# Seven products for the last two row pairs of a down projection, their block sums prepared early

## The chip, the core and the metric

The kernel runs on one core of a Trainium2 chip. The metric is the device time of one execution, in microseconds (us). TensorE (PE in the profile; PEld is its weight load) multiplies, VectorE (DVE) and ScalarE (ACT) do the element-wise work, GpSimd (POOL) and SyncE (SP) issue the DMA transfers: POOL those that accumulate or run on the software queue, SP those on a hardware queue. Each engine works through its own instructions in the order in which the program gives them and waits on semaphores; an issue that waits on SP holds up every later issue on SP.

## The reference

One decoder layer on x of 256 tokens by 2048, float32:

- proj = x @ W_in, split among 8 differential-attention heads and 8 MoBA heads (with 256 tokens MoBA has one block, so it is causal attention), each with partial rotary embedding;
- mix = heads @ W_out; h = LayerNorm(2^0.25 * x + mix);
- u = h @ W_up (2048 by 11264), g and val its halves; act = silu(causal depthwise conv of width 3 over g) * val (256 by 5632);
- out = LayerNorm(2^0.25 * h + act @ W_down), with W_down 5632 by 2048.

## The kernel before

**Precision.** Each float32 operand is split in two float32r parts, `hi` (a ScalarE copy) and `lo` (operand minus hi, on VectorE). A product then takes three: hi by hi, hi by lo, lo by hi. The split tiles come from rings of six `hi` and six `lo` tiles of 128 x 1024 (`splits`). For half of each `k` weight of the differential heads the subtraction is done in another way (`by_dma`): ScalarE writes minus the operand's hi part, and an accumulating DMA on POOL's queue adds the operand.

**Stages.** A list `stream` holds one entry for each weight tile (1 MB): 16 `v` steps, 32 `q`/`k` steps (16 heads, from index `first_q` = 16), 16 `o` steps (from `first_o` = 48), 88 up steps (from `first_u`), and 8 down steps (from `first_d`). Step i multiplies tile i, while the tiles after it are split and those further on are loaded: `begin(i)` and `middle(i)` split tiles i + 2 and i + 3, and `begin(i)` loads tile i + 6. Loads go out on SP into `raw` buffers. There are four, handed out in turn (`raw_tile`, list `turn`); a load waits until the buffer's last reader, the split of the tile that had it before, is done.

**The down projection.** W_down is cut into 22 pairs of 128 rows, p = 0 to 21, and two column halves, n = 0 and 1, of 1024. A pair times a half can be done with eight block products of 128 x 128 by 128 x 512 (24 products with the split), or with seven (21, a Strassen scheme) if sums of the weight blocks and of the activation blocks are made first. Beside the up steps, pairs 0 to 19 run with seven products (the `jobs`): the activations of a pair are spilled to DRAM (`dparts`, `dsums`) and read back for the other half. What is left stands in the eight down steps, called d0 to d7 here:

| step | pair | column half | products |
|---|---|---|---|
| d0, d1 | 20, 21 | n = 0 | 24 each |
| d2, d3 | 20, 21 | n = 1 | 24 each |
| d4 to d7 | 16 to 19 | n = 1 | 24 each, in a last phase ordered by output block |

d0 is the profile's work from 1049.22 us on. In the last phase, token rows 0 to 127 come first: for each of the two column blocks d4, d5, d6, d7 with six products each. Activations of d4 to d7 come back from DRAM (`act_back`, into the tile `back`, and for d7 into `slot`). Column half 0 is finished after d1: `shared_out` and `z_add` add its banks to the residual `z` on VectorE. The gain and bias of the last LayerNorm (2 MB, spread over all partitions) are loaded by `load_gb(2, ...)` into the place of the tile `tslot`. One of the four `raw` buffers serves the jobs during the up steps; it is put back at the head of the turn in the last up step (`turn.insert(0, ...)`), where d4's load takes it.

**What sets the order.** All of it is written out by hand: a dictionary `after` of functions by step, and the order of calls in `up_step`, `begin` and `middle`. A tile with the same tag as an older one waits until every reader and writer of the older one is done, also those that the program issues later.

Of the kernel before, what the change touches and what calls it, by code (L numbers as in the profile page):

```python
# [11 lines left out]
F32 = mybir.dt.float32  # L12
# [39 lines left out]
SEGMENTS = 5  # L52

SEVEN = {"v": ((5,), range(1, 8, 3)), "d": ((), ()), "o": ((3, 6), (3,))}

ORDER = {"v": (1, 0, 2, 3), "d": (0, 1, 2, 3), "o": (2, 0, 1, 3)}

# [5 lines left out]
def hymba_layer(ctx: ExitStack, tc: tile.TileContext, a: dict):  # L63
# [60 lines left out]
            turn.append(n)  # L124
        return keep.tile([P, 2048], F32, name="raw", tag=f"raw{n}"), n

    def load_down(t, p, n):
# [3 lines left out]
        SP.dma_start(b[:, 0:4:3], src[0])  # L131
        SP.dma_start(b[:, 1:3], src[1])

    def load(i):
        if i >= NS or i in loaded or (i, 0) in parts:
            return
        loaded[i] = t = raw_tile()[0]
        if i < 2:

            for k in range(2):  # L140
                load_x(2 * i + k, 2 * i + k + 1)
                for c in range(2):
                    o = i % 2 * 1024 + k * 512
                    SP.dma_start(t[:, c * 1024 + k * 512:c * 1024 + k * 512 + 512], a["w_v"][c, 0][:, o:o + 512])  # L144
            return
        if stream[i][0] == "d":
            load_down(t, *stream[i][1:3])
            return
        for x, y in pieces(i):
            if stream[i][0] == "v":  # L150

                _, p, n, _ = stream[i]
                if n == 0 and x < 1024:
                    load_x(*rows_of(p, x, y))
                o = p % 2 * 1024 + x % 1024
                SP.dma_start(t[:, x:y], a["w_v"][2 * n + x // 1024, p // 2][:, o:o + y - x])
            else:
                SP.dma_start(t[:, x:y], stream[i][3][:, x:y])
# [28 lines left out]
    def split_hi(i, half):  # L187
        if i >= NS or (i, half) in parts:
            return
        o = MOVE_AT if stream[i][0] in "vod" or i - first_u in (0, 1) else 0  # L190
        hi, lo = (splits.tile([P, 1088], F32R, name=n)[:, o:o + 1024] for n in ("hi", "lo"))
        t = loaded[i] if half == 0 else loaded.pop(i)
        ACT.activation(hi, t[:, half * 1024:half * 1024 + 1024], AF.Copy)  # L193
        parts[i, half] = (hi, lo)
        waiting[i, half] = t

    def split_lo(i, half):
        if (i, half) in waiting:
            hi, lo = parts[i, half]
            t = waiting.pop((i, half))  # L200
            DVE.tensor_tensor(lo, t[:, half * 1024:half * 1024 + 1024], hi.bitcast(F32), ALU.subtract)  # L201

    def split_first(i):

# [17 lines left out]

    x2 = keep.tile([P, KT, 2, S], F32R, name="x2", tag="t2")
    xh, xl = x2[:, :, 0], x2[:, :, 1]
    z = keep.tile([P, 2, D], F32, name="z")
    xraw = z.rearrange("p t d -> p (t d)")
# [260 lines left out]
    def load_gb(which, both):  # L487
        for j, n in enumerate(("g", "b")):
            t = both[:, j]
            src = a[f"ln{which}_{n}"]  # L490
            SP.dma_start(t, bass.AP(tensor=src.tensor, offset=src.offset, ap=[[0, P], [1, D]]))
            gb[n] = t
# [37 lines left out]
    def act_back(i):  # L530

        if i >= NS or stream[i][2] == 0 or stream[i][1] >= PT - LATE:
            return
        _, p, _, j = stream[i]
        if "back" not in kept:
            kept["back"] = keep.tile([P, 4, 4, S], F32R, name="back", tag="big")
        t = down_slot()[:, 14:].rearrange("p a (b t) -> p (a b) t", t=S) if i == NS - 1 else kept["back"][:, j % 4]
        POOL.dma_start(t, kept["parts"][p])
# [35 lines left out]
    def act_out(f, u):  # L574
        DVE.tensor_tensor(act_pair(f // 2)[:, f % 2], u, gates.pop(f), ALU.mult)
# [192 lines left out]
                then[m]()  # L768


    side, raw0 = {}, {}

    jobs = [(0, p, 4 * p + 8, 4) for p in range(PART)]
# [101 lines left out]
    for kind, pairs in (("v", VP), ("d", PT)):  # L875
        for n in range(2):
            np_ = pairs - (PAIRED_END + PART * (SEGMENTS - 1) if kind == "d" and n == 1 else 0)
            n7 = 2 * PART if kind == "d" and n == 0 else len(SEVEN[kind][n])
# [34 lines left out]
    def begin(i):  # L913

        urgent(i)
        j = i + 2
        if j < NS and seven(j):
            blocks_raw(j)
            act_sums(j)
        elif j - 1 < NS and seven(j - 1):  # L920
            blocks_sum(j - 1, 1)
            if j - 1 >= VP:
                split(j, 1)
            blocks_hi(j - 1, 1)
# [12 lines left out]
        if i >= first_d:  # L937
            act_back(i + 3)
        load(i + 6)
        pending(i)  # L940
# [21 lines left out]
    def pending(i):  # L962
        for x in after.pop(i, ()):
            if x[0] == LATER:
                x[2](*x[3])

    def done(i):
        for half in range(2):
# [94 lines left out]
    for i in range(first_o):  # L1063
        begin(i)
        if i < first_q:
            run_v(i)
        else:
            run_a(i)
        if i == 8:
            load_consts()  # L1070
        if i == 11:
            lambdas()
        if i == 14:
            SP.dma_start(z, a["x"])
        if i == 14:
            load_table("cos_m")
            load_table("sin_m")
# [33 lines left out]
    for i in range(first_o, last[0]):  # L1111
# [33 lines left out]
    assert not [k for k in after if k <= last[0]], after  # L1145

    h2 = keep.tile([P, KT, 2, S], F32R, name="h2", tag="t2")
    hh, hl = h2[:, :, 0], h2[:, :, 1]
# [235 lines left out]
    def up_step(i):  # L1384
# [24 lines left out]
            early_copies(turning, step)  # L1409
        if carried:  # L1410
            carried.pop()()
        split_hi(i + 2, 0)
        behind = 0 <= turning < SEGMENTS - 1 and step == 3
        if 2 in now and behind:
            r_hi(j, 1, 3)
# [21 lines left out]
            t_hi(3, side["f"][0])  # L1437
        if 0 in new:
            s_lo(1)
        split_hi(i + 2, 1)  # L1440
        if behind:
            up_copy(i)
        if s % 2 == 1 and u is not None:
# [59 lines left out]
        if 2 in now and j == len(jobs) // 2 * 2 - 1:  # L1503

            turn.insert(0, side["raw"][1])
            load(i + 5)
# [19 lines left out]

    for i in range(first_u + 2, first_d):
        up_step(i)
    act_out(FT - 1, up_sum(first_d - 1))
    split_act(first_d + 1, 1)  # L1530

    def z_stats(t, c, w):

# [25 lines left out]
    for i in range(first_d, NS - PAIRED_END):  # L1559
        begin(i)  # L1560
        _, p, n, j = stream[i]
        if i == last[0] - 1:
# [6 lines left out]
            for t in range(2):  # L1569
                for c in range(2):  # L1570
                    z_stats(t, c, (512, 256)[t])
        if seven(i):
            mm_seven(i)
        else:
            for k in range(2):
                mm_d(i, 0, [0, 1], k)
            if n == 0 and p == PT - 1:
                for c in range(2):
                    z_add(0, 0, c, CB[0][c])
            elif i < last[0] - 1:  # L1580
                middle(i)
            for k in range(2):
                mm_d(i, 1, [0, 1], k)
            done(i)
            if n == 0 and p == PT - 1:
                for c in range(2):
                    z_add(0, 1, c, CB[1][c])
                middle(i)
        for k in range(2):
            aparts.pop((i, k))  # L1590

# [171 lines left out]
```

## Time and profile before

| | us |
|---|---|
| median of 3 runs (1104.05 to 1104.23) | 1104.17 |
| the profiled execution | 1104.46 |
| its span, first to last instruction | 1102.7 |
| TensorE busy | 1094.2 |
| VectorE busy | 946.7 |
| ScalarE busy | 721.7 |
| POOL busy | 71.2 |

Times in the profile count from the first instruction. A row of the timeline is: start, duration, engine, line, operation, tiles written <- read, shapes, count, and in brackets the idle time of the engine before it with what ended it. A merged row's duration runs from the first start to the last end. A row of the stretches is: the stretch, its length, the busy time of PE, PEld, DVE, ACT and POOL (with instruction counts), the granted TensorE clock, the busy share of the 16 DMA engines, and GB/s. A row of groups is: line, engine, operation, tiles, shapes, count, then busy us and mean ns of one, then idle time before. A DMA's row shows its issue, not its landing.

### The profile page before, as it was taken

Reading aid. Unit: us, or ns where it says so; the run is one execution under the profiler, and the core shown is the slowest. Engines: PE = TensorE matmul, PEld = TensorE weight load, DVE = VectorE, ACT = ScalarE, POOL = GpSimd, SP = SyncE. Lnnn points to the kernel's source line nnn. Section 1 sums busy time; section 2 is a strip of 40 time slices with the busy share of each in tenths; the row PEclk is TensorE's granted clock in tenths of the full one; section 3 lists DMA queues with packets and bytes.
Section 4 is the critical chain, followed back from the end, with each engine's and each line's share of the span. In section 5 each row is a group of like instructions: output and inputs, shape, how many; then the busy total and the mean of one; then the engine's idle time right before and its main releaser. Section 6 shows DMA issues by size and latency. Waiting matters only on the chain.

```text
span 1102.7 us, 16138 instructions
## 1 busy us (share of the span) xinstructions
PE 1094.2 (99%) x5884; PEld 944.0 (86%) x5884; DVE 946.7 (86%) x1613; ACT 721.7 (65%) x1166; POOL 71.2 (6%) x99
## 2 busy tenths in 40 slices
PE   9999999999999999999999999999999999999997
PEld 6888888888888898888888888888888888888886
DVE  6987778887789979888999989998899988999876
ACT  6765676655475486666666767677776767677652
POOL 0100110000000000000000000000100000000003
PEclk9999999999999999999999999999999999999999
DMA  9899876444467557988988888989898889888772
GB/s 330 271 278 307 253 224 209 156 153 153 160 204 256 185 206 227 289 276 269 311 276 291 284 291 322 305 306 308 283 275 277 303 309 308 298 275 279 209 292 77
DMA packets 64336, 283.54 MB, mean 257 GB/s; under 512 B 6576, under 2 KB 8064, under 8 KB 46464
## 3 DMA queue, kind: packets, MB, share of 16 engines
q1 hardware_dynamic: 53456, 235.57, 58.0%
q0 software_dynamic: 10656, 46.67, 19.0%
q8 instruction: 46, 0.75, 0.3%
q14 instruction: 34, 0.28, 0.1%
q10 hardware_dynamic: 144, 0.26, 0.1%
HBM read 233.69 MB, written 20.97 MB: 231 GB/s over the span
## 4 chain that ended last, share of the span: by engine, by line
PE 98%; DMA 0%; DVE 0%; ACT 0%; SPq 0%; issue 0%; DVEq 0%
PE bank L282 97%; DMA raw<-in_w_v 0%; PE bank L428 0%; PE bank L1162 0%; PE bank L475 0%; DVE z L1611 0%; DVE z L1607 0%; ACT hi L213 0%; DVE st L499 0%; PE bank L1201 0%; DVE z L496 0%; SPq L144 0%; SPq L229 0%; DVE mv L505 0%; ACT ms L1676 0%
## 5 line engine op out<-in xcount | busy, mean ns | idle before, releaser
L282 PE MATMUL bank<-h,hi 128*128 128x512 f32 x1376 | 480.9, 390 | 0.0
L282 PE MATMUL bank<-h,lo 128*128 128x256 f32 x1376 | 387.9, 282 | 0.0
L282 PEld LDWEIGHTS bank<-h,hi 128*128 128x128 f32 x1376 | 258.3, 188 | 54.7
L282 PEld LDWEIGHTS bank<-h,lo 128*128 128x128 f32 x1376 | 259.9, 189 | 3.6
L201 DVE TENSOR_TENSOR lo<-raw,hi 128x1024 fp32r<-128x1024 f32 x173 | 210.4, 1219 | 13.9 <-ACT hi L193 13.6
L193 ACT ACTIVATE hi<-raw 128x1024 fp32r<-128x1024 f32 x173 | 180.6, 1048 | 6.9 <-PE bank L282 6.9
L282 PE MATMUL bank<-x,hi 128*128 128x512 f32 x512 | 182.9, 398 | 0.0
L184 DVE TENSOR_TENSOR lo<-raw,hi 128x1024 fp32r<-128x1024 f32 x115 | 137.5, 1221 | 40.9 <-ACT hi L182 40.7
L182 ACT ACTIVATE hi<-raw 128x1024 fp32r<-128x1024 f32 x123 | 127.6, 1055 | 44.3 <-PE bank L282 21.8
L282 PE MATMUL bank<-x,lo 128*128 128x256 f32 x512 | 144.2, 282 | 0.0
L841 ACT ACTIVATE tslot<-tf 128x512 fp32r<-128x512 f32 x144 | 88.4, 627 | 62.8 <-DVE tf L1477 23.8
L282 PEld LDWEIGHTS bank<-x,hi 128*128 128x128 f32 x512 | 96.2, 188 | 20.6 <-issue 1.0
L844 DVE TENSOR_TENSOR tslot<-tf,tslot 128x512 fp32r<-128x512 f32 x144 | 97.5, 688 | 11.1 <-ACT tslot L841 10.6
L282 PEld LDWEIGHTS bank<-x,lo 128*128 128x128 f32 x512 | 96.8, 189 | 0.2
L1288 ACT ACTIVATE ub<-bank 128x512 f32<-128x512 f32 x86 | 50.7, 590 | 69.7 <-PE bank L282 69.7
L282 PE MATMUL bank<-hi,x 128*128 128x512 f32 x192 | 52.0, 393 | 0.6 <-ACT hi L213 0.6
L282 PE MATMUL bank<-tslot,more 128*128 128x512 f32 x192 | 49.1, 391 | 0.0
L1297 DVE TENSOR_TENSOR ub<-ub 128x256 f32<-128x256 f32 x86 | 36.1, 420 | 12.3 <-ACT ub L1288 12.2
L1426 POOL DMA_DIRECT2D rslot<-raw x18 | 15.8, 879 | 466.6 <-ACT sp L847 466.6
L562 ACT ACTIVATE gc<-ub,vec 128x256 f32<-128x256 f32 x43 | 25.8, 599 | 29.9 <-DVE ub L1297 29.8
L282 PE MATMUL bank<-tslot,sp 128*128 128x512 f32 x180 | 45.0, 391 | 0.0
L282 PEld LDWEIGHTS bank<-hi,x 128*128 128x128 f32 x192 | 36.3, 189 | 8.8 <-ACT hi L213 1.3
(277 smaller groups left out, 1660.5 us busy)
## 6 DMA issues: line engine op xcount, KB each, us to landing
raw<-in_w_u SPq DMA_DIRECT2D x88, 1024.0 KB, 6.9
raw<-in_w_qk SPq DMA_DIRECT2D x32, 1024.0 KB, 5.0
raw<-in_w_d SPq DMA_DIRECT2D x52, 512.0 KB, 6.6
ring<-in_w_d SPq DMA_DIRECT2D x36, 512.0 KB, 6.0
raw<-in_w_o SPq DMA_DIRECT2D x16, 1024.0 KB, 4.9
raw<-in_w_v SPq DMA_DIRECT2D x28, 512.0 KB, 7.3
rslot<-raw POOLq DMA_DIRECT2D x18, 768.0 KB, 7.0
dparts<-rslot SPq DMA_DIRECT2D x20, 512.0 KB, 8.5
```

Source lines behind the costliest of these rows:

```text
L182: ACT.activation(hi[:, s], t[:, x:y], AF.Copy)
L184: DVE.tensor_tensor(lo[:, s], t[:, x:y], hi[:, s].bitcast(F32), ALU.subtract)
L193: ACT.activation(hi, t[:, half * 1024:half * 1024 + 1024], AF.Copy)
L201: DVE.tensor_tensor(lo, t[:, half * 1024:half * 1024 + 1024], hi.bitcast(F32), ALU.subtract)
L282: PE.matmul(out, lhsT, rhs, start=start, stop=stop)
L562: ACT.activation(gates[f], g, AF.Identity, bias=vec[:, C_CB + f:C_CB + f + 1], scale=vec[:, C_W + 2 * FT + f:C_W + 2 * FT + f + 1])
L841: ACT.activation(side["t"][:, 0, j], f, AF.Copy)
L844: DVE.tensor_tensor(side["t"][:, 1, j], f, side["t"][:, 0, j].bitcast(F32), ALU.subtract)
L1288: ACT.activation(t.rearrange("p j t -> p (j t)"), up_bank(i), AF.Copy)
L1297: DVE.tensor_tensor(u[:, 0], u[:, 0], u[:, 1], ALU.add)
L1426: POOL.dma_start(side["r"][:, 1], w[:, 0:3], accum_op=ALU.add)
```

## The change

- d0 and d1 use seven products: 21 instead of 24 (`mm_ready`). The sums of their weight blocks, with their splits, are made during the MoBA heads: for each of the two, from steps `first_q` + 18 and + 25 on, two loads of 0.5 MB, four sums, four splits, and four stores of 0.5 MB to a DRAM tensor (`tsums`). The place of `z` serves as buffer.
- `z` (the residual x, 2 MB) is therefore loaded at step `first_o` - 1 instead of 14.
- To make room on VectorE, half of `k` is split by DMA for the MoBA heads too.
- Before d0 and d1 the prepared blocks are fetched, 2 MB each: d0's on POOL's queue into four `splits` tiles, d1's on SP into `slot` after the up steps. A quarter of their raw weights is no longer loaded. d3's and d5's loads move behind d1's fetch, d4's stays in the last up step.
- d1 is split after the up steps, and the sums of the activations of rows 20 and 21 are made there.
- `act_back` moves from POOL's queue to SP's. `load_gb(2, ...)` moves from the last up step to the end of step d1.
- In step d1, d3's split moves behind the products and the three additions to `z` that follow them.

```diff
-        return kind == "k" and h < NDIFF and half == 1
+        return kind == "k" and half == 1
...
-        POOL.dma_start(t, kept["parts"][p])
+        SP.dma_start(t.bitcast(F32), kept["parts"][p].bitcast(F32))
...
+    def ready_load(c):
+        if c == 0:
+            ready["w"] = keep.tile([P, 4096], F32, name="prep", tag="z")
+            ready["dram"] = dram.tile([len(READY), P, 8, 512], F32R, name="tsums")
+        kind, p, n = READY[c]
+        for k in range(2):
+            SP.dma_start(ready["w"][:, k * 1024:k * 1024 + 1024], a["w_d"][2 * p + 1 - k][:, n * 1024:(n + 1) * 1024])
...
+    for c in range(len(READY)):
+        base = first_q + READY_AT + READY_STEP * c
+        for step, fn, args in ((0, ready_load, (c,)), (2, ready_sums, (0,)), (2.5, ready_hi, (0,)), (3, ready_sums, (1,)),
+                               (3.5, ready_hi, (1,)), (4, ready_lo, (0,)), (5, ready_lo, (1,)),
+                               (5, ready_store, (c, 0)), (6, ready_store, (c, 1))):
+            extra.setdefault(base + step, []).append((fn, args))
...
+    def mm_ready(i, order, then={}):
...
+        pairs = ((0, 0), (0, 1), (1, 0))
+        steps_ = [(m, y) for m in order[:3] for y in pairs]
+        steps_ += [(m, y) for m in order[3:] for y in pairs if y[1] == 0] + [(m, (0, 1)) for m in order[3:]]
...
-        else:
+        elif j != first_d + LATE + 1:
             split(j, 0)
             split(j, 1)
...
+        if i == first_o - 1:
+            z = keep.tile([P, 2, D], F32, name="z")
+            SP.dma_start(z, a["x"])
...
             turn.insert(0, side["raw"][1])
             load(i + 5)
-        load(i + (5 if len(turn) == 3 else 6))
-        if i == first_d - 1:
-            load_gb(2, keep.tile([P, 2, D], F32, name="gb2", tag="ma"))
+        if i < first_d - 2:
+            load(i + (5 if len(turn) == 3 else 6))
+        if i == first_d - 2:
+            ready_fetch(first_d, [splits.tile([P, 1088], F32R, name=n)[:, MOVE_AT:MOVE_AT + 1024]
+                                  for n in ("hi", "hi", "lo", "lo")])
...
     for i in range(first_u + 2, first_d):
         up_step(i)
+    down_act_sums(PT - 2)
     act_out(FT - 1, up_sum(first_d - 1))
     split_act(first_d + 1, 1)
+    ready_fetch(first_d + 1, [down_slot()[:, 0:8]])
+    for j in range(3, 6):
+        load(first_d + j)
+    split_hi(first_d + 1, 0)
...
+    late_sums(PT - 2, keep.tile([P, 4, S], F32R, name="sp", tag="four"))
+    split_hi(first_d + 1, 1)
+    for j in range(2):
+        split_lo(first_d + 1, j)
+    down_act_sums(PT - 1)
+    kept["back"] = keep.tile([P, 4, 4, S], F32R, name="back", tag="big")
+    late_sums(PT - 1, kept["back"][:, 1])
...
-        if seven(i):
-            mm_seven(i)
+        if i == first_d:
+            mm_ready(i, (1, 2, 3, 4, 5, 7, 6))
+        elif n == 0:
+            mm_ready(i, (1, 2, 3, 4, 5, 7, 6), {m: lambda t=t, c=c: z_add(0, t, c, CB[t][c])
+                                                for m, t, c in ((2, 0, 0), (3, 0, 1), (4, 1, 0))})
+            for k in range(2):
+                split(i + 2, k)
+            middle(i)
+            load_gb(2, keep.tile([P, 2, D], F32, name="gb2", tag="ma"))
```

More of the change, by code (lines that the diff above doesn't have):

```diff
@@ L125, in raw_tile, with load_down @@
         return keep.tile([P, 2048], F32, name="raw", tag=f"raw{n}"), n
-    def load_down(t, p, n):
+    def load_down(t, p, n, short=False):
         b = t.rearrange("p (b c) -> p b c", c=512)
         src = [a["w_d"][2 * p + k][:, n * 1024:(n + 1) * 1024].rearrange("p (b c) -> p b c", c=512) for k in range(2)]
-        SP.dma_start(b[:, 0:4:3], src[0])
+        if short:
+            SP.dma_start(b[:, 0], src[0][:, 0])
+        else:
+            SP.dma_start(b[:, 0:4:3], src[0])
         SP.dma_start(b[:, 1:3], src[1])
@@ L146, in load @@
         if stream[i][0] == "d":
-            load_down(t, *stream[i][1:3])
+            load_down(t, *stream[i][1:3], ready_of(i) is not None)
             return
@@ L192, in split_hi @@
         t = loaded[i] if half == 0 else loaded.pop(i)
-        ACT.activation(hi, t[:, half * 1024:half * 1024 + 1024], AF.Copy)
+        w = 512 if half == 1 and ready_of(i) is not None else 1024
+        ACT.activation(hi[:, 0:w], t[:, half * 1024:half * 1024 + w], AF.Copy)
         parts[i, half] = (hi, lo)
-        waiting[i, half] = t
+        waiting[i, half] = t, w
     def split_lo(i, half):
@@ L199, in split_lo @@
             hi, lo = parts[i, half]
-            t = waiting.pop((i, half))
-            DVE.tensor_tensor(lo, t[:, half * 1024:half * 1024 + 1024], hi.bitcast(F32), ALU.subtract)
+            t, w = waiting.pop((i, half))
+            DVE.tensor_tensor(lo[:, 0:w], t[:, half * 1024:half * 1024 + w], hi[:, 0:w].bitcast(F32), ALU.subtract)
     def split_first(i):
@@ L224, in hymba_layer @@
     xh, xl = x2[:, :, 0], x2[:, :, 1]
-    z = keep.tile([P, 2, D], F32, name="z")
-    xraw = z.rearrange("p t d -> p (t d)")
+    xraw = keep.tile([P, 2 * D], F32, name="xraw", tag="z")
     def load_x(k0, k1):
@@ L768, in mm_seven, with ready_of @@
                 then[m]()
+    ready, extra = {}, {}
+    def ready_of(i):
+        kind, p, n, _ = stream[i]
+        return READY.index((kind, p, n)) if (kind, p, n) in READY else None
+    def ready_load(c):
[5 more added lines that the diff above has]
+            SP.dma_start(ready["w"][:, k * 1024:k * 1024 + 1024], a["w_d"][2 * p + 1 - k][:, n * 1024:(n + 1) * 1024])
@@ new lines, in ready_pair, with ready_sums @@
+    def ready_pair(j):
+        w = ready["w"]
+        return (w[:, 2048:3072], w[:, 3072:]) if j == 0 else (w[:, 1024:2048], w[:, 0:1024])
+    def ready_sums(j):
+        b = ready["w"].rearrange("p (b c) -> p b c", c=512)
+        if j == 0:
+            DVE.tensor_tensor(b[:, 4], b[:, 2], b[:, 3], ALU.subtract)
+            DVE.tensor_tensor(b[:, 5], b[:, 3], b[:, 1], ALU.add)
+        else:
+            DVE.tensor_tensor(b[:, 2], b[:, 1], b[:, 4], ALU.subtract)
+            DVE.tensor_tensor(b[:, 3], b[:, 0], b[:, 2], ALU.subtract)
@@ new lines, in ready_hi, with ready_lo, ready_store @@
+    def ready_hi(j):
+        x, hi = ready_pair(j)
+        ACT.activation(hi.bitcast(F32R), x, AF.Copy)
+    def ready_lo(j):
+        x, hi = ready_pair(j)
+        DVE.tensor_tensor(x.bitcast(F32R), x, hi, ALU.subtract)
+    def ready_store(c, j):
+        x, hi = (y.rearrange("p (b c) -> p b c", c=512) for y in ready_pair(j))
+        dst = ready["dram"][c]
+        SP.dma_start(dst[:, 2 * j:2 * j + 2].bitcast(F32), hi)
+        SP.dma_start(dst[:, 4 + 2 * j:6 + 2 * j].bitcast(F32), x)
+    for c in range(len(READY)):
[4 more added lines that the diff above has]
+            extra.setdefault(base + step, []).append((fn, args))
@@ new lines, in ready_fetch @@
+    def ready_fetch(i, tiles):
+        src = ready["dram"][ready_of(i)]
+        if len(tiles) == 1:
+            for j in range(2):
+                SP.dma_start(tiles[0][:, 4 * j:4 * j + 4].bitcast(F32), src[:, 4 * j:4 * j + 4].bitcast(F32))
+            ready[i] = [(tiles[0][:, j], tiles[0][:, 4 + j]) for j in range(4)]
+            return
+        for j, t in enumerate(tiles):
+            POOL.dma_start(t.rearrange("p (b c) -> p b c", c=512).bitcast(F32), src[:, 2 * j:2 * j + 2].bitcast(F32))
+        ready[i] = [tuple(tiles[y][:, x:x + 512] for y in (j // 2, 2 + j // 2)) for j, x in enumerate((0, 512) * 2)]
@@ new lines, in mm_ready @@
+    def mm_ready(i, order, then={}):
+        kind, p, n, _ = stream[i]
+        sh, sl = shares(ready["s", p])
+        (s3, s1), (s2, s4) = ([(sh[j][:, k], sl[j][:, k]) for k in range(2)] for j in range(2))
+        (h0, l0), (h1, l1) = aparts[i, 0], aparts[i, 1]
+        a11, a12, a22 = (h0[:, 0:P], l0[:, 0:P]), (h1[:, 0:P], l1[:, 0:P]), (h1[:, P:], l1[:, P:])
+        w = [weights(i, 512 * b, 512) for b in range(3)]
+        ts = ready.pop(i)
+        ms = {5: (s1, ts[0]), 7: (s3, ts[1]), 6: (s2, ts[2]), 4: (a22, ts[3]), 1: (a11, w[0]), 2: (a12, w[1]), 3: (s4, w[2])}
+        pairs = ((0, 0), (0, 1), (1, 0))
+        steps_ = [(m, y) for m in order[:3] for y in pairs]
+        steps_ += [(m, y) for m in order[3:] for y in pairs if y[1] == 0] + [(m, (0, 1)) for m in order[3:]]
+        final = {m: x for x, (m, _) in enumerate(steps_)}
+        for x, (m, y) in enumerate(steps_):
+            t, c = {2: (0, 0), 3: (0, 1), 4: (1, 0)}.get(m, (None, None))
+            key, dst = ((kind, n, m), MB[m]) if t is None else ((kind, n, t, c), CB[t][c])
+            lhs, rhs = ms[m]
+            mm_count(key, dst, lhs[y[0]], rhs[y[1]])
+            if m in then and x == final[m]:
+                then[m]()
+        done(i)
@@ L877, in hymba_layer @@
             np_ = pairs - (PAIRED_END + PART * (SEGMENTS - 1) if kind == "d" and n == 1 else 0)
-            n7 = 2 * PART if kind == "d" and n == 0 else len(SEVEN[kind][n])
+            n7 = 2 * PART + LATE if kind == "d" and n == 0 else len(SEVEN[kind][n])
             if kind == "d" and n == 0:
@@ L965, in pending @@
                 x[2](*x[3])
+        for fn, args in extra.pop(i, ()):
+            fn(*args)
     def done(i):
@@ L1072, in hymba_layer @@
             lambdas()
-        if i == 14:
-            SP.dma_start(z, a["x"])
         if i == 14:
@@ L1144, in hymba_layer @@
                 at(first_o + 9 + n // 2, z_piece, n // 2, n % 2, bank[n], 1, 512, 1.0)
-    assert not [k for k in after if k <= last[0]], after
+    assert not [k for k in (*after, *extra) if k <= last[0]], (after, extra)
     h2 = keep.tile([P, KT, 2, S], F32R, name="h2", tag="t2")
@@ L1411, in up_step @@
             carried.pop()()
-        split_hi(i + 2, 0)
+        if i < first_d - 1:
+            split_hi(i + 2, 0)
         behind = 0 <= turning < SEGMENTS - 1 and step == 3
@@ L1439, in up_step @@
             s_lo(1)
-        split_hi(i + 2, 1)
+        if i < first_d - 1:
+            split_hi(i + 2, 1)
         if behind:
@@ L1528, in hymba_layer, with late_sums @@
         up_step(i)
+    down_act_sums(PT - 2)
     act_out(FT - 1, up_sum(first_d - 1))
     split_act(first_d + 1, 1)
+    ready_fetch(first_d + 1, [down_slot()[:, 0:8]])
+    for j in range(3, 6):
+        load(first_d + j)
+    split_hi(first_d + 1, 0)
+    def late_sums(p, sp):
+        ready["s", p] = sp
+        side["sh"], side["sl"] = shares(sp)
+        for j in range(2):
+            s_hi(j)
+        for j in range(2):
+            s_lo(j)
+    late_sums(PT - 2, keep.tile([P, 4, S], F32R, name="sp", tag="four"))
+    split_hi(first_d + 1, 1)
+    for j in range(2):
+        split_lo(first_d + 1, j)
+    down_act_sums(PT - 1)
+    kept["back"] = keep.tile([P, 4, 4, S], F32R, name="back", tag="big")
+    late_sums(PT - 1, kept["back"][:, 1])
     def z_stats(t, c, w):
@@ L1576, in hymba_layer @@
                 mm_d(i, 0, [0, 1], k)
[L1577 to L1580, printed above, removed]
+            if i < last[0] - 1:
                 middle(i)
@@ L1584, in hymba_layer @@
             done(i)
[L1585 to L1588, printed above, removed]
         for k in range(2):
```

3 lines of the change are left out of this document (2 added, 1 removed).

## The prediction

> **What bounds the kernel now.** I read the page first (busy shares, chain), then the chain in order of time, then TensorE's timeline around the changed steps, then the engines' stretches, and last the queues.
>
> ```profile
> span 1102.7 us, 16138 instructions
> PE 1094.2 (99%) x5884; PEld 944.0 (86%) x5884; DVE 946.7 (86%) x1613; ACT 721.7 (65%) x1166; POOL 71.2 (6%) x99
> ...
> 402.17 691.11 PE bank L282 x3708
> 1093.28 0.02 issue
> ...
> 1049.22 0.62 PE L282 MATMUL bank<-hi,ends 128*128 128x512 f32 x2
> ...
> 1070.98 0.39 PE L282 MATMUL bank<-hi,back 128*128 128x512 f32 x1
> ```
>
> TensorE is the bound: from 402 us its products follow each other without a hole until 1093.28. So each product taken away is worth its start-to-start distance, and each wait put in front of TensorE costs its full length. The two rows at 1049.22 and 1070.98 are the starts of d0 and d4 (names as in the section on the kernel); between them lie four steps of 24 products: 21.76 / 96 = 0.2267 us each.
>
> **Products removed.** d0 and d1 go from 24 to 21 products: 6 x 0.2267 = -1.36 us. That is all the change can bring. In the new order d1 would start at 1053.98, d2 at 1058.74, d3 at 1064.18, and the last phase at 1069.62, whose first six products are d4's; d5's activations ("back") are read after them, at 1070.98.
>
> **MoBA heads: sums made early.** Rows: one pair of steps with a MoBA head, one with a differential head (which already splits half of `k` by DMA), columns us, busy PE, PEld, DVE, ACT, POOL, clock, DMA share, GB/s; then the groups that price the additions.
>
> ```profile
> 234.87:247.61 12.74, 12.74 (x78) 11.37 (x76) 10.36 (x22) 6.43 (x12) 0.00 (x0) 1.00 0.47 165
> 155.20:167.50 12.30, 12.30 (x78) 11.02 (x76) 9.99 (x26) 9.02 (x23) 1.61 (x2) 1.00 0.74 218
> ...
> L184 DVE TENSOR_TENSOR lo<-raw,hi 128x1024 fp32r<-128x1024 f32 x25 | 30.0, 1220 | 9.5 <-ACT hi L182 9.5
> L182 ACT ACTIVATE hi<-raw 128x1024 fp32r<-128x1024 f32 x24 | 25.4, 1057 | 10.8 <-issue 8.1 <-PE bank L282 2.7
> L676 DVE TENSOR_TENSOR tf<-raw 128x512 f32<-128x512 f32 x1 | 0.7, 684 | 0.0
> ```
>
> VectorE loses 8 subtractions (8 x 1.22 = 9.8 us) and gets per row pair 4 sums and 2 subtractions (4 x 0.684 + 2 x 1.22 = 5.2), 10.4 in all: even. ScalarE gets 8 + 4 copies of 1.06 us, 12.7 us over 102 us, with 6.3 us free in every 12.74. The DMA engines get 8 accumulates of 0.5 MB, 2 MB of loads and 4 MB of stores, at a share of 0.47. In the row of 155.20 such accumulates run at a share of 0.74 and TensorE is busy for all 12.30 us. Cost 0; cover: VectorE's 2.4 us and the DMA engines' half. Without cover it would be at most the third sum's wait for its load, about 1 us.
>
> **z's load moved from step 14 to step 47.** It is 2 MB, waits on SP for the stores of the last prepared block, and stands ahead of the `w_o` loads.
>
> ```profile
> 301.20 0.33 SPq L158 DMA_DIRECT2D raw<-in_w_o  x1
> ...
> 321.27 0.86 POOL L675 DMA_DIRECT2D oslot<-raw  x1 [16.01 <-ACT oslot L674]
> ...
> raw<-in_w_qk SPq DMA_DIRECT2D x32, 1024.0 KB, 5.0
> ```
>
> The load behind it is issued at 301.20 and first read some 2 us before the accumulate of 321.27. It lands within 5.0 us unhindered; 2 MB ahead of it cost some 5.3 us at 400 GB/s. It lands at about 311: hidden, with 8 us left. `z` itself is first read in step 55. Cost 0.
>
> **The turn from up to down steps.** The sums of rows 20 and 21 and the split of d1 now run after the last up step.
>
> ```profile
> 1043.28 1.05 ACT L1523 ACTIVATE rslot<-raw 128x1024 fp32r<-128x1024 f32 x1
> 1044.23 0.70 ACT L596 ACTIVATE ends<-ring 128x256 fp32r<-128x256 f32 x2
> 1048.24 0.42 ACT L596 ACTIVATE ah<-ring 128x256 fp32r<-128x256 f32 x1 [0.95 <-DVE ring L575]
> 1048.68 1.28 ACT L1544 ACT_TABLE_LOAD   x1
> ...
> L850 DVE TENSOR_TENSOR sp<-sf,sp 128x256 fp32r<-128x256 f32 x4 | 1.7, 418 | 0.0
> L855 DVE TENSOR_TENSOR sf<-ring 128x256 f32<-128x256 f32 x1 | 0.4, 415 | 0.0
> L856 DVE TENSOR_TENSOR sf<-sf,ring 128x128 f32<-128x128 f32 x1 | 0.3, 291 | 0.0
> L857 DVE TENSOR_TENSOR sf<-ring,sf 128x128 f32<-128x128 f32 x1 | 0.3, 291 | 0.0
> ```
>
> ScalarE after 1048.6 (each row's start to the next start: 0.95 for 1024 columns, 0.35 for 256): d1's first half, then the two sums of row 20, ready at 1050.3. TensorE wants them after six products, at 1050.58. VectorE's two subtractions (0.42 each) end at about 1050.8 against 1051.04. Cost 0, margin 0.2; if missed, below 0.5 us.
>
> **Fetches.** The rows: POOL's last accumulate of the up steps, its time to landing (median), and the last use of h2's step.
>
> ```profile
> 1035.64 0.88 POOL L1426 DMA_DIRECT2D rslot<-raw  x1 [29.42 <-ACT sp L847]
> ...
> rslot<-raw POOLq DMA_DIRECT2D x18, 768.0 KB, 7.0
> ...
> 1046.49 0.85 PE L282 MATMUL bank<-tslot,rslot 128*128 128x512 f32 x3
> ```
>
> d0's 2 MB stand on POOL in place of d3's load, behind that accumulate, so they move from 1042.6. With 0.5 MB of spilled activations and d4's 1 MB beside them, 3.7 MB at 0.4 MB per us, all has landed at 1051.8; the last block is wanted after 17 products of d0, at 1053.1. d1's 2 MB leave SP when h2 is free (1046.49, the up products' end). `hi` is wanted at 1056.0 and `lo` at 1057.8; behind the above they land at about 1054.4 and 1057.0. Cost 0, ends 0 and 2 us.
>
> **Down steps: the queue of SP.** Here I expect the loss. The rows: SP's issues before, POOL's issues before, then VectorE.
>
> ```profile
> 1047.38 0.33 SPq L491 DMA_DIRECT2D gb<-in_ln_g  x1
> 1058.12 0.38 SPq L131 DMA_DIRECT2D raw<-in_w_d  x1
> ...
> 1049.90 1.61 POOL L538 DMA_DIRECT2D back<-dparts  x3 [13.38 <-PE bank L282]
> ...
> 1055.73 2.36 DVE L184 TENSOR_TENSOR lo<-raw,hi 128x1024 fp32r<-128x1024 f32 x2 [2.20 <-ACT hi L182]
> 1063.55 1.28 DVE L1319 TENSOR_TENSOR z<-z,bank 128x512 f32<-128x512 f32 x2
> 1071.54 2.35 DVE L184 TENSOR_TENSOR slot<-raw,slot 128x1024 fp32r<-128x1024 f32 x2
> 1073.81 2.35 DVE L184 TENSOR_TENSOR end<-raw,end 128x1024 fp32r<-128x1024 f32 x2
> 1069.70 2.01 ACT L182 ACTIVATE end<-raw 128x1024 fp32r<-128x1024 f32 x2 [0.28 <-DMA raw<-in_w_d]
> ```
>
> Before, the four activation fetches leave an otherwise idle POOL at 1049.9, and d7's load is issued at 1058.12, when d3's split has ended (1055.73 + 2.36). After, SP issues in this order: d3, d5, d6, back of d4, d7, gain and bias (2 MB), back of d5, of d6, of d7. And d7's load changes its buffer. d4 is now loaded before d3, so the turn of the four buffers gives d7 the one of d4: the load waits for d4's split, and everything behind it on SP waits too.
>
> When is d4 split? VectorE, in order: sums and split of d1 and the sums of row 21 until about 1054.4 (1.22 + 0.69, 1.0, 0.84, with ScalarE's copies between); d2's split behind ScalarE's table load, until 1058.8; three additions to z (0.64 each) until 1060.7; d3's and d4's splits, 4 x 1.18, until 1065.4. The lower end comes from TensorE: the third addition needs product 18 of d1, at 1053.98 + 18 x 0.2267 = 1058.06; one addition and four splits later it is 1063.4. I take 1065.4, since ScalarE is serial there.
>
> What is then on the way? d7's megabyte, 5.0 us by the row above: 1070.4. Gain, bias and d5's half megabyte, 2.62 MB, at the rate of these stretches:
>
> ```profile
> 1055.00:1060.00 5.00, 5.00 (x24) 4.14 (x23) 3.56 (x4) 1.65 (x2) 0.00 (x0) 1.00 1.06 408
> 1060.00:1065.00 5.00, 5.00 (x24) 4.14 (x23) 4.93 (x7) 2.49 (x3) 0.00 (x0) 1.00 1.09 397
> ```
>
> 2.62 / 0.402 = 6.5 us: d5's activations land at 1076.9 and TensorE wants them at 1070.98. Stall 5.9 us. The ends: release at 1063.4 gives 3.9; a d7 load as slow as before (1058.12 to 1069.70, 11.6 us) gives 12.5. I take 5.9, because the engines have little else left by then. d6's and d7's activations follow 1.3 us apart, as fast as TensorE uses them (1.36).
>
> **The clock after such a hole.** Rows: the first products, the last ones, the last window.
>
> ```profile
> 1.20 4.45 PE L282 MATMUL bank<-idle 128*128 128x512 bf16 x10 [1.20 <-DVE idle L902]
> 5.08 1.64 PE L282 MATMUL bank<-hi,x 128*128 128x512 f32 x4
> 6.56 0.62 PE L282 MATMUL bank<-lo,x 128*128 128x512 f32 x2
> ...
> 1093.11 1.88 PE L282 MATMUL bank<-z,ident 128*128 128x512 f32 x4
> ...
> 1097.00:1102.00 5.00, 0.00 (x0) 0.00 (x0) 1.26 (x2) 0.86 (x2) 0.00 (x0) 0.61 0.58 211
> ```
>
> The mean of 0.61 in the last window is full clock for about 1.1 us and half after, so the clock fell at 1098.1, 3.1 us after the dense products ended (1094.99). A hole of 5.9 us is longer. Coming back, the first ten products of the kernel start 0.388 us apart and the next four 0.37, against 0.2267: 14 products lose 1.6 to 2.2 us. I take 1.9.
>
> [...]
>
> **The sum.** -1.36 + 5.9 + 1.9 = +6.4 us. The profiled run took 1104.46 us with a span of 1102.7, 0.29 over the median of 1104.17; against the median: 1110.6 us, +0.6%.
>
> **Rivals.**
> 1. The hole comes but the clock stays full: +4.5, 1108.7 us. For it: 5.9 is only twice 3.1, and one early activation shortens it.
> 2. The activations are in time, VectorE is not. Before, d7's first `lo` is ready at 1075.0 (1073.81 + 1.2) and wanted at 1075.3. After, VectorE still has eight additions (0.64) and d5's split (2.35) behind 1065.4 and reaches d6 at 1072.9, 1.3 later than before, while TensorE is 1.36 earlier: a stall of 1.3 + 1.36 - 0.3 = 2.4, 1105.2 us. This decides only if the activations land before 1073.4.
> 3. Not slower: d7's load finds its buffer free before 1070.98 - 6.5 - 5.0 = 1059.5, and nothing is late: 1102.8 us. Against it: product 18 of d1 ends at 1058.06 and d3's and d4's splits are yet to come.
> 4. d1's fetch is late by 2 us as well: d4's split moves along, 1112.6 us.
>
> **Chances.** Forecast 0.44, rival 1 0.25, rival 2 0.08, rival 3 0.10, rival 4 with larger stalls 0.10, and 0.03 for a gain above the six products that I can't name. 0.2% (2.2 us) is about what a measurement of this kernel tells from no change. Slower is forecast, rivals 1 and 4: 0.79; within: rivals 2 and 3, 0.18; faster 0.03. The range goes from just under rival 2 (1104.4) to rival 4 with a late release (1114.0); the forecast with rival 1 alone spans 1106.7 to 1113.
>
> **What would show it.** TensorE idle for some 6 us near 1071, waiting for "back"; a granted clock below 1 just after; SP's back issues behind gain and bias, after a d7 load issued near 1065; no idle TensorE in the MoBA heads or between 1049 and 1069. It is wrong if d7's load is issued before 1060, or if the hole stands elsewhere.

## The result: slower by 0.8%, and the profile after

The changed kernel takes 1112.51 us (1111.35 to 1116.44), the kernel before, on the same chip, 1104.27 (1104.05 to 1104.6): a ratio of 1.0079, 95% interval 1.0064 to 1.0095. Forecast were 1110.6 us and a range of 1104.4 to 1114.0. The profiled execution of the changed kernel took 1111.35 us, 6.89 more than the profiled one before; it is the quickest of the six, so what the median has above it stands in no trace.

One correction comes first, since it bears on the reading. In the listing of the change, `load(i + 5)` behind `turn.insert(0, ...)` stands as kept, and the text says that d4's load stays in the last up step. In the changed kernel that line is gone: d4's load moves behind d1's fetch too, and the order there is d3, d4, d5. So d3, not d4, takes the buffer that is put back at the head of the turn, and d7's load waits for d3's split. The prediction was built on the wrong order.

The page of the changed kernel (span and engines), and from its chain of waits the pieces around the longest one (start us, us, what):

```profile
span 1109.6 us, 16224 instructions
PE 1095.4 (99%) x5878; PEld 943.8 (85%) x5878; DVE 947.8 (85%) x1626; ACT 732.9 (66%) x1182; POOL 78.3 (7%) x107
...
1066.47 11.61 DMA back<-dparts
1078.08 0.14 issue
1078.21 22.42 PE bank L288 x114
```

PE's busy time is much as before, yet the chain no longer runs through TensorE alone: it crosses a transfer of d5's activations that takes 11.61 us. TensorE's timeline in the heads, at d2's start and in the last phase (start us, us, line, operation, count, and in brackets the idle time and what ended it):

```profile
272.24 0.28 PE L288 MATMUL bank<-x,lo 128*128 128x256 f32 x1
273.79 0.70 PE L434 MATMUL bank<-ident,e 128*128 128x128 f32 x3 [1.28 <-DVE e L428]
...
1060.56 1.06 PE L288 MATMUL bank<-hi,ends 128*128 128x512 f32 x2 [0.58 <-DVE z L1410]
...
1073.02 0.39 PE L288 MATMUL bank<-hi,back 128*128 128x512 f32 x1
1078.21 0.77 PE L288 MATMUL bank<-hi,back 128*128 128x512 f32 x1 [4.81 <-DMA back<-dparts]
1078.78 0.63 PE L288 MATMUL bank<-lo,back 128*128 128x512 f32 x1
1079.21 1.05 PE L288 MATMUL bank<-hi,back 128*128 128x512 f32 x2
```

Three waits, of which one was forecast. Between starts, and less the usual distance of 0.2267 us in the down steps, they cost 1.6 us in the heads, 1.1 at d2 (two gaps) and 4.97 in the last phase. Then the products are 0.427 us apart (1079.21 to 1080.06 for two) until about 1081.2, some 1.5 us lost. The stretches say the same in their columns of granted clock, DMA share and GB/s (the last three):

```profile
1070.00:1075.00 5.00, 3.41 (x16) 2.48 (x14) 4.93 (x7) 2.33 (x3) 0.00 (x0) 1.00 1.01 419
1075.00:1078.00 3.00, 0.00 (x0) 0.00 (x0) 3.00 (x3) 0.00 (x0) 0.00 (x0) 0.97 1.01 404
1078.00:1081.50 3.50, 3.29 (x8) 2.68 (x9) 2.70 (x7) 0.31 (x1) 0.00 (x0) 0.54 0.17 65
```

Added up: the six products -1.36, heads +1.6, d2 +1.1, hole +4.97, clock +1.5, a start that was 0.57 earlier in this execution and an end some 0.4 shorter: +6.8 of 6.89 us. Between these places TensorE has no hole, as in these two stretches (the first after the heads' wait, the second to the end of the up steps):

```profile
275.00:400.00 125.00, 124.99 (x651) 107.12 (x650) 110.87 (x186) 74.47 (x122) 4.57 (x6) 1.00 0.71 234
400.00:1040.00 640.00, 640.00 (x3461) 556.15 (x3460) 575.08 (x918) 448.66 (x675) 39.19 (x57) 1.00 0.85 285
```

And SP's queue in the down steps (timeline, issues only):

```profile
1059.84 0.38 SPq L137 DMA_DIRECT2D raw<-in_w_d  x1
...
1060.83 0.38 SPq L544 DMA_DIRECT2D back<-dparts  x1
1063.90 0.38 SPq L137 DMA_DIRECT2D raw<-in_w_d  x1
...
1064.85 0.42 SPq L497 DMA_DIRECT2D gb<-in_ln_g  x1
1065.31 1.11 SPq L497 DMA_DIRECT2D gb<-in_ln_b  x1
1066.47 0.91 SPq L544 DMA_DIRECT2D back<-dparts  x2
```

In order: d6's weights, d4's activations, then 3 us of nothing while d7's load waits for d3's split, then d7, gain, bias, and only then the activations of d5 and d6.

### The profile page after: what moved, and what is told of

It is laid out like the page before. It is cut to its first block, busy times and chain, and to the rows that moved or that the text cites. A ratio compares the mean times of both kernels' runs of the same rounds, so it can differ in the third digit from the quotient of the medians.

```text
span 1109.6 us, 16224 instructions
## 1 busy us (share of the span) xinstructions
PE 1095.4 (99%) x5878; PEld 943.8 (85%) x5878; DVE 947.8 (85%) x1626; ACT 732.9 (66%) x1182; POOL 78.3 (7%) x107
## 5 line engine op out<-in xcount | busy, mean ns | idle before, releaser
L208 DVE TENSOR_TENSOR lo<-raw,hi 128x1024 fp32r<-128x1024 f32 x173 | 209.2, 1212 | 14.1 <-ACT hi L200 13.7
L190 DVE TENSOR_TENSOR lo<-raw,hi 128x1024 fp32r<-128x1024 f32 x107 | 128.0, 1220 | 37.0 <-ACT hi L188 36.6
L932 DVE TENSOR_TENSOR tslot<-tf,tslot 128x512 fp32r<-128x512 f32 x144 | 97.5, 687 | 11.2 <-ACT tslot L929 10.7
```

The source lines that it names most:

```text
L190: DVE.tensor_tensor(lo[:, s], t[:, x:y], hi[:, s].bitcast(F32), ALU.subtract)
L208: DVE.tensor_tensor(lo[:, 0:w], t[:, half * 1024:half * 1024 + w], hi[:, 0:w].bitcast(F32), ALU.subtract)
L932: DVE.tensor_tensor(side["t"][:, 1, j], f, side["t"][:, 0, j].bitcast(F32), ALU.subtract)
```

## The experiments

Times are medians; each ratio is against the kernel before, measured beside it. Each edit is to the changed kernel unless it says otherwise.

### 1. Gain and bias behind the activations (e1_gain_last)

```diff
-            load_gb(2, keep.tile([P, 2, D], F32, name="gb2", tag="ma"))   # end of step d1
+            load_gb(2, keep.tile([P, 2, D], F32, name="gb2", tag="ma"))   # after act_back(last[3])
```

> The changed kernel with one issue moved: gain and bias are loaded behind the activations of d5 to d7 on SP instead of ahead of them. Theory (order on SP's queue makes the hole): d5's activations have 2.1 MB less ahead of them, 5.2 us at 0.4 MB per us, and land at about 1072.9 where TensorE wants them at 1073.2; the hole of 4.97 us shrinks to less than 1 us, the clock stays full (1.5 us more), so 1112.5 - 6.5 = about 1106 us. Rival (the added 3.5 MB make the last transfers late in any order): the hole moves to d7's weights or to gain and bias, and the time stays above 1110 us.

1106.56 us (1105.97 to 1110.26), ratio 1.003 [1.0019, 1.004]. One line moved on SP's queue takes away 6 of the 8.2 us: the hole and the half clock are gone (the mean clock of the profile is 0.999, of the changed kernel's 0.996). What is next in line there is a split of d7 (TensorE's timeline):

```profile
1077.63 1.43 PE L288 MATMUL bank<-end,slot 128*128 128x512 f32 x5 [0.60 <-DVE end L190]
```

Between starts it costs 0.77. With heads 1.7 and d2 1.1 that is -1.36 + 3.6 = +2.2, and the profiled execution is at 1106.42, 1.96 above the one before.

### 2. The activations back on POOL's queue (e2_back_on_pool)

```diff
-        SP.dma_start(t.bitcast(F32), kept["parts"][p].bitcast(F32))
+        POOL.dma_start(t, kept["parts"][p])
```

> The changed kernel with the activations of d4 to d7 on POOL's queue again. Theory (order on SP): they are issued before 1060 and land before 1070; no hole at the activations; the VectorE splits of d6 and d7 come next and cost 0 to 2.4 us; 1105.5 to 1108 us. Rival (volume): they take turns with SP's loads, so d7's load lands 1.5 MB / 0.4 = 3.9 us later than now (1071.8), TensorE waits for its split some 3 us, the clock may fall, 1109 to 1111 us.

1112.99 us (1111.53 to 1115.14), ratio 1.0081 [1.0065, 1.0096]: nothing is gained, and the theory that a queue of their own makes the activations timely and the kernel quick fell. They are timely; other things are late. POOL's issue, ScalarE's copy of d3, and two of TensorE's waits (timelines):

```profile
1053.31 1.59 POOL L544 DMA_DIRECT2D back<-dparts  x3 [9.10 <-ACT hi L200]
...
1065.23 2.01 ACT L188 ACTIVATE hi<-raw 128x1024 fp32r<-128x1024 f32 x2 [4.52 <-DMA raw<-in_w_d]
...
1076.97 0.50 PE L288 MATMUL bank<-lo,back 128*128 128x512 f32 x1 [0.97 <-DVE lo L190]
...
1081.90 2.50 PE L288 MATMUL bank<-slot,back 128*128 128x512 f32 x5 [3.27 <-DVE slot L190]
```

2 MB of activations are on the way from 1053 on, beside SP's weights, and d3's weights are the ones that lose: ScalarE waits 4.52 us for them. Behind the last of these waits five products take 2.50 us, against 1.43 in experiment 1's row, and in the heads the clock halved (0.50 from 276 to 279 us, last section); the mean clock of the profile is 0.993. Between starts the two stretches cost some 4.5 us of this profile's 10.7 above the one before.

### 3. The hole filled with products that serve for nothing (e3_filled_hole)

```diff
+            if c == 0 and i == last[1]:      # last phase, ahead of d5
+                for _ in range(18):
+                    mm(MB[1], aparts[last[0], 0][0][:, 0:P], weights(last[0], 0, 512)[0], True, True)
```

> The changed kernel with 18 products more (18 x 0.227 = 4.1 us) into an unused bank, between d4's and d5's products of the last phase, where TensorE stands idle for 4.97 us. Theory (the clock falls in the hole and costs 1.5 us after it): the granted clock stays full, the products behind the hole start 0.227 us apart instead of 0.427, and the time falls by about 1.5 us, to 1111 us. Rival (the slow products cost nothing, since the activations of d6 and d7 are awaited anyway): the time stays at 1112.5 us.

1111.02 us (1109.59 to 1113.28), ratio 1.0063 [1.0048, 1.0078]; the profiled execution 1109.59, 1.76 below that of the changed kernel. TensorE's timeline:

```profile
1072.74 4.47 PE L288 MATMUL bank<-hi,back 128*128 128x512 f32 x19
1077.85 0.47 PE L288 MATMUL bank<-hi,back 128*128 128x512 f32 x1 [0.64 <-DMA back<-dparts]
1078.16 0.39 PE L288 MATMUL bank<-lo,back 128*128 128x512 f32 x1
```

The activations come at the same time, but the product behind them is short (0.39, not 0.63) and the next ones are 0.227 apart; the mean clock of the profile is 0.999, against 0.996. So the clock's share of the loss is about 1.5 us, as expected; the two ranges of times overlap, so it rests on the rows.

### 4. The sums in the heads, one to two steps earlier (e4_sums_earlier)

```diff
-READY_AT, READY_STEP = 18, 7
+READY_AT, READY_STEP = 16, 8
```

> The changed kernel with the preparation of rows 20 and 21 begun at steps first_q + 16 and + 24 instead of + 18 and + 25, so that the second pair's load is issued two steps after the first pair's last store and on a step whose load does not wait for an accumulate. Theory (VectorE stands 5.7 us for the second pair's load, which makes the one wait of TensorE in the heads): TensorE's wait of 1.6 us at 272 goes, VectorE's wait falls below 2 us, 1112.5 - 1.6 = 1110.9 us. Rival (the heads lack VectorE or DMA time as a whole): the wait turns up at another head, and the time stays at 1112.5 us.

1112.56 us (1112.18 to 1112.62), ratio 1.0074 [1.0057, 1.0091]: no gain. The wait at 272 us goes, and one of 1.3 us comes around 220 us, where the first pair's sums now fall among the last differential heads and VectorE has nothing free. Of the 1.6 us that were expected some 0.4 are left in TensorE's heads, and the mean clock of this profile is 0.995, against 0.996 of the changed kernel's.

### 5. The heads' load ahead of the step's weight load (e5_load_first, with 1)

```diff
+        for fn, args in extra.pop(("first", i), ()):   # ready_load
+            fn(*args)
         load(i + 6)
```

> e1 (gain and bias last) with one more edit: the preparation's two loads per row pair go out on SP at the head of their step, ahead of that step's weight load, which waits for an accumulating DMA. Theory (VectorE's 5.7 us for the second pair's load come from that place in SP's queue): the loads of row 21 are issued some 4 us earlier, near 258 us, VectorE waits below 2 us and TensorE's wait of 1.5 us at 272 is gone: 1106.5 - 1.5 = 1105.0 us, and the spread of the runs (1106 to 1110 in e1) narrows, if it comes from the clock falling in that wait. Rival (e4: the heads lack VectorE time, the wait only moves): a wait of 1 us or more stays between 210 and 300, 1106 us.

1106.33 us (1105.31 to 1108.83), ratio 1.0024 [1.0015, 1.0034]: the same as experiment 1 within the intervals. The theory was that the second pair's load is late because it stands behind a weight load that waits for a split by DMA. SP's own waits from 255 to 265 us (us in total, times, longest), first of the changed kernel, then of this one:

```profile
SPq L164 <- DMA lo<-raw: 10.7, 1, 10.7
SPq L789 <- DMA tsums<-prep: 0.7, 1, 0.7
```

```profile
SPq L789 <- DMA tsums<-prep: 12.1, 2, 11.3
```

With the wait in front taken away, the load waits just as long for something else: the first pair's stores to DRAM, out of the buffer that it wants to fill. It was a second wait, hidden behind the first, and the load goes out at 262.2 us in the one and 262.4 in the other. That is why the heads lack cover. TensorE's wait there was 0.9 us in this profile against 1.7 in experiment 1's, but 2.0 in experiment 7's, which has the same load. In the changed kernel VectorE then stands in the sum (timeline), and the head's own `e` behind it:

```profile
270.91 0.69 DVE L798 TENSOR_TENSOR prep<-prep 128x512 f32<-128x512 f32 x1 [5.74 <-DMA prep<-in_w_d]
```

### 6. The order at the turn and in d1 (e6_turn_order, with 1)

```diff
+        elif i == first_d:                      # d2's copies only
+            split_hi(j, 0)
+            split_hi(j, 1)
...
-    ACT.activation(root, eps, AF.Sqrt)
...
+            ACT.activation(root, eps, AF.Sqrt)  # behind step d0
...
+            def then_z(m, t, c):                # in step d1
+                z_add(0, t, c, CB[t][c])
+                if m == 3:
+                    for k in range(2):
+                        split_lo(first_d + 2, k)
```

> e1 with two edits at the turn: d2's subtractions stand behind the first two additions to z on VectorE instead of ahead of all three, and the activation table's load stands behind d2's copies on ScalarE. Theory (VectorE's order makes d2's wait of 1.1 us and, through its backlog, the 0.77 us at d7): both waits go, VectorE reaches d6 some 1.9 us earlier, 1106.5 - 1.9 = 1104.6 us. Rival (VectorE has too much to do there in any order): d2's wait turns into a wait for d2's subtractions or grows at d7, 1106 us or more.

1107.7 us (1105.25 to 1108.98), ratio 1.0031 [1.0018, 1.0044], where about 1104.6 was expected. The wait at d2 is gone, which shows its cause: VectorE did d2's subtractions, which waited for ScalarE, ahead of the additions that free TensorE's banks. (The table load, which held ScalarE up for 1.28 us, moved with them; the two edits were not separated.) The wait at d7 is gone as well, but that shows less, since the new wait below may give VectorE the time. In the changed kernel (VectorE's timeline):

```profile
1057.45 2.36 DVE L190 TENSOR_TENSOR lo<-raw,hi 128x1024 fp32r<-128x1024 f32 x2 [2.03 <-ACT hi L188]
1059.73 1.88 DVE L1410 TENSOR_TENSOR z<-z,bank 128x512 f32<-128x512 f32 x3
```

But TensorE, now earlier, waits 1.2 us for d5's activations, and the profiled execution lost 2.5 us to the wait in the heads, with a half clock behind it (0.51 from 276.0 to 279.5 us).

### 7. 5 and 6 together (e7_both)

> The edits of e1, e5 and e6 together. Theory: the changed kernel's waits were all made by the order of its queues, so what is left is the six products: 1104.2 - 1.36 = 1102.8 us, just below the kernel before, with the spread of the kernel before. Rival (some of the waits belong to the added work itself): above 1104.2 us.

1106.45 us (1104.25 to 1107.58), ratio 1.0022 [1.0013, 1.0031]; 1102.8 was expected. In its profile 2.0 us stay in the heads (the load of experiment 5 is no earlier) and 1.6 for d5's activations.

### 8. What the products are worth (e8_six_less: the kernel before, six products of d0 and d1 left out)

```diff
+        if (kind, n, t, c, k) == ("d", 0, 1, 1, 1):
+            continue
```

> The kernel before with six products of d0 and d1 left out and nothing else changed: it leaves out one of the eight blocks of each of these two pairs. Theory (six products are all that there is to gain): between 1102.8 us (1104.2 - 6 x 0.2267) and, since VectorE's last splits were only 0.3 us ahead of TensorE at d7, 1103.9 us. Rival (there is more to gain than the products' own time): below 1102.5 us.

1102.83 us (1102.52 to 1103.19), ratio 0.9989 [0.998, 0.9999]. 1.2 of 1.36 us arrive when nothing is added in return. This is the most that the change could bring.

### 9. The heads' work spread out (e9_heads_spread, with 1 and 6)

```diff
-READY_AT, READY_STEP = 18, 7
+READY_AT, READY_STEP = 16, 8
-        for step, fn, args in ((0, ready_load, (c,)), (2, ready_sums, (0,)), ...
+        for step, fn, args in ((0, ready_load, (c,)), (3.5, ready_sums, (0,)), ...
```

The loads go out as in experiment 4, but the first sum follows 3.5 steps behind its load instead of 2, the stores 6.5 and 7 instead of 5 and 6.

> Gain and bias last (e1), the order at the turn (e6), and another timetable in the heads instead of e5's edit: the first row pair's loads at step 32 with its sums from 35.5 on, the second's loads at step 40 with its sums from 43.5 on, so that the first pair's last stores are issued two steps ahead of the second pair's loads into the same buffer. Theory (the second load waits for those stores to land, 11 to 13 us; VectorE then waits for the load): no wait of TensorE above 0.3 us between 200 and 310; what is left is the wait for d5's activations seen in e6 (1.2 us) and e7 (1.6): 1104.1 - 1.36 + 1.5 = 1104.2 us, with a spread below 1 us. Rival (VectorE is short of time in the heads): a wait of 0.5 us or more at 220 or 272, 1105 us and more.

1104.3 us (1103.51 to 1106.38), ratio 1.0004 [0.9995, 1.0013]. The heads' wait is gone (stretch of this kernel):

```profile
260.00:275.00 15.00, 15.00 (x91) 13.43 (x90) 11.36 (x24) 9.77 (x16) 0.86 (x1) 1.00 0.95 327
```

So the load's late landing was its cause: it goes out 3.9 us earlier (258.35 against 262.21) and has 1.5 steps more until the sum, and VectorE doesn't stand in the sum. Experiment 4, with the early load alone, still had 1.8 us of that wait on VectorE, but none of TensorE there; what the spreading adds is the place at 220 us, where the first pair's sums no longer cost TensorE anything. The version is 3.4 us below experiment 6, which differs only in the timetable. Left is the wait for d5's activations:

```profile
1072.74 0.47 PE L288 MATMUL bank<-hi,back 128*128 128x512 f32 x1 [1.70 <-DMA back<-dparts]
```

### 10. d5's activations ahead of d7's load (e10_d5_first, with 9)

```diff
-        if i >= first_d:
+        if i >= first_d and i != first_d + 2:
             act_back(i + 3)
+        if i == first_d + 1:
+            act_back(i + 4)
```

> e9 with one more edit: d5's activations go out on SP ahead of d7's load instead of behind it. Theory A (only the order on SP is left): d5's wait goes and nothing takes its place, 1102.8 to 1103.2 us. Theory B (VectorE is the next bound there: it has the sums and splits of d1 to do in the turn and reaches d6 and d7 some 1.5 us later than in the kernel before): d5's wait goes, a wait of 1 to 2 us for the splits of d6 or d7 takes its place, and the time stays at 1104.2 us.

1103.9 us (1103.44 to 1104.56), ratio 0.9998 [0.9989, 1.0007]: level with the kernel before, and the best version found. Neither theory named what followed: d5 is in time, and d6's activations are late.

```profile
1073.12 1.62 PE L288 MATMUL bank<-slot,back 128*128 128x512 f32 x6 [0.94 <-DMA back<-dparts]
```

A likely reason is in the last two columns (DMA share, GB/s) of the stretches around the down steps, first of the kernel before, then of this one:

```profile
1060.00:1070.00 10.00, 10.00 (x46) 8.29 (x45) 9.40 (x12) 6.69 (x8) 0.00 (x0) 1.00 0.82 306
1070.00:1075.00 5.00, 5.00 (x24) 4.14 (x23) 4.97 (x7) 1.91 (x3) 0.00 (x0) 1.00 0.01 2
1040.00:1078.00 38.00, 38.00 (x176) 31.73 (x175) 28.78 (x40) 19.12 (x25) 2.14 (x4) 1.00 0.75 268
```

```profile
1060.00:1070.00 10.00, 10.00 (x46) 8.28 (x45) 9.86 (x12) 6.44 (x7) 0.00 (x0) 1.00 1.03 387
1070.00:1075.00 5.00, 4.06 (x18) 2.77 (x16) 4.97 (x7) 2.01 (x2) 0.00 (x0) 1.00 1.04 423
1040.00:1078.00 38.00, 37.06 (x170) 30.36 (x169) 30.73 (x48) 20.34 (x28) 0.47 (x1) 1.00 0.99 376
```

Before, 268 GB/s over 38 us are 10.2 MB, and by 1070 the engines are done. After, 376 GB/s are 14.3 MB, and they are full to the end: 4.1 MB more in the same 38 us take up the whole spare quarter.

### 11. d6's activations ahead of d7's load too (e11_backs_first, with 10)

```diff
+        if i == first_d + 1:
+            for j in range(4, 7):
+                act_back(first_d + j)
```

> e10 with d6's activations ahead of d7's load too (1 MB more ahead of it than in e9, 2.6 us). Theory A (only the order on SP is left): no wait above 0.3 us in the last phase, 1102.8 to 1103.1 us. Theory B (the DMA engines are full from 1045 to 1075 in e10, so what goes first makes the next thing late): d7's weights land some 1.3 us later than in e10, TensorE waits 0.5 to 1.5 us for d7's split in place of the 0.94 us for d6's activations, and the time stays at 1103.4 to 1104.2 us.

1104.93 us (1104.01 to 1106.68), ratio 1.0007 [0.9998, 1.0016]. If only the order were wrong, this would be the fix. Instead the waits move on to what now comes behind (TensorE's timeline, then ScalarE's copies of d7):

```profile
1072.59 1.43 PE L288 MATMUL bank<-slot,back 128*128 128x512 f32 x5 [0.45 <-DVE slot L190]
1074.37 0.47 PE L288 MATMUL bank<-end,slot 128*128 128x512 f32 x1 [0.34 <-DMA slot<-dparts]
1075.43 1.45 PE L288 MATMUL bank<-end,slot 128*128 128x512 f32 x5 [0.59 <-DVE end L190]
...
1073.06 2.01 ACT L188 ACTIVATE end<-raw 128x1024 fp32r<-128x1024 f32 x2 [4.45 <-DMA raw<-in_w_d]
```

Of the orders tried, none puts everything in time. That the volume is too much for the stretch in any order is argued from the full shares, not shown. Nor is it the only bound: the first of these waits, 0.6 us between starts, is for VectorE, which waited for nothing before it and was busy for 14.25 of the 14.50 us from 1059.10 on.

## Why the prediction was right, and where it was not

**What held.** The direction, and the mechanism behind its largest part: d5's activations stand on SP behind d7's load and behind gain and bias, TensorE waits for them in the last phase, and the clock halves (0.50 from 1078 to 1081 us). Experiment 1 shows the queue's order as the cause, experiment 3 the clock. The six products are worth what was said (1.36 by count, 1.2 in experiment 8). `z`'s load (SP waits 9.1 us at its line, TensorE not at all), the turn and both fetches cost 0.

**The hole: 5.9 forecast, 4.97 measured, by errors that cancel.** The step "d7's load changes its buffer" failed: it waits for d3's split, not d4's, and went out at 1063.90, not 1065.4. The step "the engines have little else left by then" failed too: from 1063.90 to the landing at 1078.08, at some 0.406 MB per us (402 to 419 GB/s), 5.8 MB moved, not the 3.62 counted. Some 1.3 MB of the rest were d6's weights and d4's activations, still on the way; most of the remainder, some 0.8 MB, were the activations of d6 and d7, issued behind d5's but moved beside them (after 1078.08 the engines had only 0.2 MB left). So the activations landed at 1078.08 instead of 1076.9. And TensorE wanted them at 1073.25 instead of 1070.98, since it had lost time in two places by then. That the two errors nearly cancel is luck.

**The heads: cost 0 forecast, 1.6 measured.** The sign "no idle TensorE in the MoBA heads or between 1049 and 1069" did not hold, here and at d2. The failed step is the cover, "VectorE's 2.4 us and the DMA engines' half", taken as means over a step. I had priced its loss, "the third sum's wait for its load, about 1 us", but not asked what holds the load back: it reuses a buffer whose stores are 11 us under way. The stretches show that the half wasn't there either: from 255 to 270 us the share was 0.98.

```profile
255.00:270.00 15.00, 15.00 (x90) 13.39 (x89) 8.86 (x19) 8.51 (x18) 0.86 (x1) 1.00 0.98 317
```

**d2: not in the sum at all, 1.1 measured.** The prediction had the order on VectorE ("d2's split behind ScalarE's table load, until 1058.8; three additions to z until 1060.7") and used it only for d3's and d4's splits. It didn't ask who waits for those additions; TensorE does.

**The clock: 1.9 forecast, 1.5 measured.** It took effect for seven to eight products, not fourteen. Rival 1 (full clock, 1108.7) is out.

**The other rivals.** Rival 2, VectorE late for d7 once the activations are in time, is what experiment 1 showed, at 0.77 us at d7 where 2.4 were worked out, and experiment 11 again, at 0.6 us at d6. Rival 3's 1102.8 was reached by no version that does the added work, though the activations were made timely: something else was late each time. Rival 4, d1's fetch late, didn't occur. The forecast was 1.9 us under the median: the two terms taken as 0 are worth 2.7, and the hole and the clock together came out 1.3 smaller; the remaining 0.5 is the balance of start, end and the spread of the runs, which no term covers.

## What to carry to other kernels

A load that is put on an in-order queue takes over every wait in front of it (here the 3 us that d7's load waits ahead of d5's activations): write the queue's order out, with the release of each waiting entry, before counting bytes. A mean DMA share below 1 is no cover for a burst (0.47 over two steps before the change, 0.98 from 255 to 270 us after it), and where an order fix only hands the wait to the next transfer, suspect the volume: compare bytes per stretch before and after (here 10.2 and 14.3 MB in 38 us), not the order again. For work put into "idle" time, ask when its buffer is free, and who stands behind its first wait on that engine.

## What was unexpected of the hardware

Taking one wait away can leave the issue where it was, because the next wait was already under way: 11.4 us on SP before and 12.1 after in experiment 5, for an issue at 262.2 and 262.4 us.

A much shorter wait than the 3.1 us of the prediction came with a half clock. In experiment 2's profile TensorE waited 2.0 us in the heads, and then:

```profile
273.00:275.00 2.00, 0.47 (x4) 0.35 (x4) 1.96 (x5) 2.00 (x3) 0.00 (x0) 1.00 1.06 311
276.00:279.00 3.00, 3.00 (x11) 2.52 (x11) 2.96 (x5) 0.70 (x1) 0.00 (x0) 0.50 0.17 38
```

Eleven products in 3 us, at a clock of 0.50; experiment 6's profile has the same at 0.51 from 276.0 to 279.5. In the profiles of the changed kernel and of experiments 1 and 7, with 1.4 to 1.8 us of wait at the same place (each of these waits, and the 2.0 us, is one gap between starts, less the usual distance of 0.12; what it cost, with the slow start behind it, is some 0.2 more), the clock stayed at 1 (1.00 from 276 to 279 us in the changed kernel and in experiment 7, a mean of 0.999 over experiment 1's profile). What decides between the two was not shown.

A half clock in some executions and not in others may be why the versions that wait in the heads around 272 us scatter by 3 to 5 us (experiment 1: 1105.97 to 1110.26) and experiment 10, which doesn't, by 1.1. The clocks of the single executions bear it out only in part: the changed kernel's slowest has 0.994 and its quickest 0.996, but one of experiment 1's at 1108.06 us has 0.999. Experiments 9 and 11, which wait in the last phase alone, scatter by 2.9 and 2.7. The link is argued, not shown.
